# Scan of a hybrid encoder block: log dt in the exponential's bias with an additive mask, weights made a slot ahead, reordered slot, native fp32 state products, first tap on ScalarE

## The chip, the cores and the metric

The kernel runs on one core of a Trainium2 chip. The metric is device time in microseconds (us). Engines are named as in the profile: PE (TensorE's matmuls; PEld is its weight loads), DVE (VectorE), ACT (ScalarE), POOL (GpSimd), SP (SyncE, which only issues DMAs here). SBUF is the on-chip working memory, PSUM the banks into which PE writes.

## The reference, cut to what matters

One encoder block: a combined input projection of 1024 tokens, then a Hyena branch, a Mamba-2 (SSD) branch and gates, their mixing and a mixture of experts. The change touches only the SSD branch and the projection loop around it:

```python
xbc = silu(centred_dwconv(p_xbc, conv_w, conv_b))          # 5 taps; xs, B, C
dt = softplus(p_dt + dt_bias)                               # (l, 2 directions, 32 heads)
a = dt * -exp(a_log)
# per direction, in 8 chunks of 128 tokens, 8 groups of 4 heads:
A_cs = cumsum(a)                                            # within a chunk
decay = exp(where(tril, A_cs[l] - A_cs[s], -inf))
y_diag = einsum(CB[l, s], decay[l, s], (xs * dt)[s])        # CB = C . B
states = einsum(B, exp(A_cs[-1] - A_cs), xs * dt)
carry = carry * chunk_decay + states                        # over the chunks
y_off = einsum(C, carry, exp(A_cs))
y = y_fwd + y_bwd + xs * d_skip;  y = y * silu(z), then an RMS norm per group
```

The Hyena projections pass through a centred convolution of 3 taps.

## The kernel before

The part in question is the function `front`, the first 1436 us. It runs over 89 **units**, each a projection of 128 columns of `w_in` (one of 64): `dt`, then for each of 8 SSD **groups** `xs0`, `xs1`, `B`, `C` (convolved), `z0`, `z1`, and between them 24 `hy` and 16 `gate` units. One unit is one **slot**. In it `proj_cm` runs 8 steps k, each of 6 matmuls of 512 columns in the reduced format fp32r (weights hi and lo by data hi and lo); `hook(k)` puts other matmuls ahead of step k. The order of every engine is written out by hand (a manual schedule): each engine runs its instructions in the order in which the code emits them. The scan of a group runs in slots of the following group: `start[g] = b` is its first slot, and `at(slot, when, f)` hangs a piece of work at a step k or at "begin", "side" (after the projection) or "end".

For chunk c, `pe1(c)` at step 4 of slot b+2+c makes C.B into bank S, the chunk's state from the weighted `xw`, and into bank O the product of C with the two carried states, as three fp32r products of 512 columns (`mm3`) of split operands (`sR`, `Chl`). `side_a(c)` after the projection masks C.B (`cbm`), advances the forward state `sF`, splits it, builds the exponent `Em` on DVE from `bcs` (the running sums A, broadcast by a DMA) and takes the exponential on ACT; POOL then multiplies the masked C.B by dt for both directions, head by head (`Wm`), adds the two, makes `yt` = xs * d and, last, weighs the next chunk's `xw` (`weigh`). `side_b` multiplies the weights by the exponential. `pe3(c)` at step 7 of the next slot applies them into bank Y, and `side_c(c)` at the begin of slot b+4+c sums the terms up. `post` convolves the unit before on DVE (`pin` to `acc...`), and `w_split` prepares the next unit's weights: `whi` on ACT, `wlo` on POOL.

At a group's end `post1` and `post2` normalise `zs` (8 scalings on ACT), transpose it and store it. Groups 1, 3 and 5 have 10 slots, the others 11, so `post2` falls into different slots of the next group. Three slots in a row, start[g] to start[g]+2, hold it together with the next group's transposes (`t1`, `t2`, `zs_tr`) and its backward states (`back`); they are called the **boundary** below, and the slots from start[g]+3 to the group's last its **middle**. Bank tags and their buffers: A (projections) 4, S 1, O 2, Y 1.

## Time and profile before

| | us |
|---|---|
| median of 3 runs (lowest 3528.78, highest 3532.55) | 3530.07 |
| the profiled execution, its time | 3534.84 |
| its span, first to last instruction | 3533.2 |

| share of the span | PE | PEld | DVE | ACT | POOL |
|---|---|---|---|---|---|
| busy | 90% | 71% | 73% | 40% | 47% |

The profiled execution is 4.8 us above the median, and 1.6 us of its time lie outside its span. [...]

### The profile page before, as it was taken

The numbers are of one execution on the slowest core, as the hardware profiler recorded it, in microseconds if no ns is written. First come the engines' busy times: TensorE is split into PE (matmuls) and PEld (weight loads), VectorE is DVE, ScalarE is ACT, GpSimd is POOL, SyncE is SP. The second block draws the span as 40 slices with busy tenths as digits, with TensorE's granted clock in tenths as the row PEclk, the third lists the DMA queues.
The fourth block names the chain that finished last, engine by engine and source line by source line (L and its number), as shares of the span: only waits on it lengthen the run. The fifth ranks groups of instructions, "written<-read, shape, count | busy, mean of one in ns | idle before, by whom it ended". The sixth has DMA issues, their size and how long they took to land. (4 is left out here: it accounts for less than half of the span.)

```text
span 3533.2 us, 42386 instructions
## 1 busy us (share of the span) xinstructions
PE 3188.0 (90%) x14923; PEld 2506.6 (71%) x14923; DVE 2590.6 (73%) x3551; ACT 1406.7 (40%) x2206; POOL 1676.7 (47%) x1480
## 2 busy tenths in 40 slices
PE   8989998989998998899999999997889888888893
PEld 6767776777777777567888888875666666666662
DVE  6787887888787878557994344657778787677786
ACT  3334333343334232322223212415656555565663
POOL 2545454555454546441110320215667667777774
PEclk9999899999999999899999999988999999899996
DMA  4323232322322322744325445327999899888894
GB/s 131 78 72 87 67 96 75 85 73 79 91 78 75 89 72 91 215 147 151 106 90 173 126 155 158 107 85 242 271 271 270 259 259 262 250 249 249 250 283 128
DMA packets 439908, 538.22 MB, mean 152 GB/s; under 512 B 24361, under 2 KB 373325, under 8 KB 430989
## 3 DMA queue, kind: packets, MB, share of 16 engines
q1 hardware_dynamic: 404717, 379.23, 36.6%
q0 software_dynamic: 33824, 152.06, 15.0%
q10 hardware_dynamic: 1152, 4.19, 0.3%
q8 instruction: 119, 1.95, 0.2%
q14 instruction: 96, 0.79, 0.1%
HBM read 430.29 MB, written 105.12 MB: 152 GB/s over the span
## 5 line engine op out<-in xcount | busy, mean ns | idle before, releaser
L170 PE MATMUL bankA<-xth,whi 128*128 128x512 f32 (+1 forms) x1424 | 470.1, 412 | 0.5 <-ACT whi L73 0.3
L170 PE MATMUL bankA<-xtl,whi 128*128 128x512 f32 (+1 forms) x1424 | 452.6, 400 | 0.0
L170 PE MATMUL bankA<-xth,wlo 128*128 128x512 f32 (+1 forms) x1424 | 449.4, 397 | 1.5 <-POOL wlo L74 1.5
L1618 DVE TENSOR_TENSOR elo<-eraw,ehi 128x2048 fp32r<-128x2048 f32 (+1 forms) x134 | 393.7, 2945 | 18.9 <-ACT ehi L1611 13.1
L1661 POOL DMA_INDIRECT scr_acc<-yo,sidx x96 | 231.1, 2407 | 275.9 <-DMA scr_acc<-yo,sidx 147.1
L1611 ACT CAST ehi<-eraw 128x2048 fp32r<-128x2048 f32 (+1 forms) x198 | 356.3, 1852 | 3.3 <-DMA eraw<-in_exp_w_gate_dram 3.3
L74 POOL TENSOR_TENSOR wlo<-wraw,whi 128x1024 fp32r<-128x1024 f32 (+1 forms) x89 | 225.4, 2532 | 278.1 <-ACT whi L73 278.1
L170 PEld LDWEIGHTS bankA<-xtl,whi 128*128 128x128 f32 (+1 forms) x1424 | 274.5, 193 | 64.1 <-DVE xtl L74 0.4
L170 PEld LDWEIGHTS bankA<-xth,wlo 128*128 128x128 f32 (+1 forms) x1424 | 272.2, 191 | 64.5 <-POOL wlo L74 2.0
L170 PEld LDWEIGHTS bankA<-xth,whi 128*128 128x128 f32 (+1 forms) x1424 | 268.2, 195 | 58.3 <-issue 5.4
L1618 POOL TENSOR_TENSOR elo<-eraw,ehi 128x2048 fp32r<-128x2048 f32 x64 | 298.1, 4658 | 15.8 <-ACT ehi L1611 14.7
L399 POOL TENSOR_SCALAR Wm<-cbm,dt 128x128 f32<-128x128 f32 x256 | 129.9, 507 | 348.2 <-DVE cbm L373 348.2
L1625 POOL DMA_INDIRECT xg<-scr_h,gidx x96 | 182.3, 1899 | 63.4 <-issue 24.3
L79 PE MATMUL bankA<-elo,xgh 128*128 128x512 f32 (+1 forms) x512 | 203.6, 398 | 8.6 <-DVE elo L1618 8.6
L78 PE MATMUL bankA<-ehi,xgh 128*128 128x512 f32 (+1 forms) x512 | 210.1, 410 | 0.0
L80 PE MATMUL bankA<-ehi,xgl 128*128 128x512 f32 (+1 forms) x512 | 203.3, 397 | 0.0
L1640 PE MATMUL bankB<-ident,xg 128*128 128x128 f32 (+3 forms) x768 | 113.4, 295 | 94.0 <-DMA xg<-scr_h,gidx 92.5
L1640 PEld LDWEIGHTS bankB<-ident,xg 128*128 128x128 f32 (+3 forms) x768 | 101.5, 198 | 122.9 <-issue 107.5
L74 DVE TENSOR_TENSOR xgl<-bankB,xgh 128x512 fp32r<-128x512 f32 (+1 forms) x128 | 81.3, 664 | 107.7 <-ACT xgh L73 106.0
L80 PE MATMUL bankA<-ehi,hb 128*128 128x512 f32 (+1 forms) x256 | 121.3, 474 | 27.0 <-DVE hb L74 26.9
L1877 DVE SCALAR_TENSOR_TENSOR lows<-lows,wt 64x256 f32<-64x256 f32 (+1 forms) x32 | 132.5, 4140 | 15.5 <-ACT lows L1876 15.5
L393 DVE SCALAR_TENSOR_TENSOR Em<-bcs,Acs,Em 128x128 f32<-128x128 f32 x256 | 140.9, 609 | 2.3
(551 smaller groups left out, 7672.7 us busy)
## 6 DMA issues: line engine op xcount, KB each, us to landing
eraw<-in_exp_w_gate_dram SPq DMA_DIRECT2D x128, 512.0 KB, 5.9
eraw<-in_exp_w_down_dram POOLq DMA_DIRECT2D x64, 1024.0 KB, 6.0
eraw<-in_exp_w_up_dram SPq DMA_DIRECT2D x128, 512.0 KB
wraw<-in_w_in_dram SPq DMA_DIRECT2D x88, 512.0 KB, 4.1
bcs<-scr_at SPq DMA_DIRECT2D x128, 256.0 KB, 5.6
scr_K<-kout SPq DMA_DIRECT2D x32, 512.0 KB, 2.8
Kt<-scr_K SPq DMA_DIRECT2D x32, 512.0 KB, 3.5
scr_gate<-accf SPq DMA_DIRECT2D x16, 512.0 KB, 4.2
```

Of the source, the lines that this page charges most:

```text
L74: (lo_eng or nc.vector).tensor_tensor(lo, src, hi.bitcast(F32), ALU.subtract)
L78: mm(out, sh, mh, start=first, stop=False)
L79: mm(out, sh, ml, start=False, stop=False)
L80: mm(out, sl, mh, start=False, stop=last)
L170: mm(ps[h], wt[:, k, :n], x[:, h * 512:(h + 1) * 512], start=(k == 0 and f == 1), stop=(k == KT - 1 and l == 1))
L393: STT(E[:, h], bcs[:, 1, h], self.A[:, c, 32 + j:33 + j], E[:, h], ALU.subtract, ALU.min)
L1611: nc.scalar.copy(whl[p][0][:, c], wraw[p][:, c])
L1618: eng.tensor_tensor(lo[:, c], wraw[p][:, c], hi[:, c].bitcast(F32), ALU.subtract)
L1625: nc.gpsimd.indirect_dma_start(out=t[:n, :], out_offset=None, in_=self.h_d, in_offset=bass.IndirectOffsetOnAxis(ap=tabs[r][s][0], axis=0))
L1640: nc.tensor.transpose(ps[:, j * P:j * P + n], free(t[:n, k:k + 1], [[8, P]]), self.ident[:n, :n])
L1661: nc.gpsimd.indirect_dma_start(out=self.acc_d, out_offset=bass.IndirectOffsetOnAxis(ap=tabs[r][s][1], axis=0), in_=y[:n, :], in_offset=Non ...
L1877: nc.vector.scalar_tensor_tensor(t[:, 0:256], t[:, 0:256], w, t[:, 256:512], ALU.mult, ALU.mult)
```

## The change

1. **dt by its logarithm.** `atr` makes A' = log(dt) corrected - A once (`self.A`). Per chunk, `side_e` adds a mask `negm` (0 or -1e30) to the broadcast sums of both directions in one DVE instruction of 1024 columns, and ACT takes eight exponentials of 128 columns (four heads, two directions) with A' as bias. The weights are E0 + E1 (`side_a`), times C.B straight from bank S (`side_b`). POOL's eight multiplications by dt and their sum, the masked C.B and the DVE exponent are gone.
2. **A slot ahead.** `side_e(c)` and `side_a(c)` run in slot b+1+c, one before `pe1(c)`; `weigh` runs two chunks ahead; `bcs` is loaded one slot earlier.
3. **Native state product.** `pe1` multiplies C by the states in plain fp32, two products of 256 columns, without splits.
4. **Reordered slot.** `post` is a generator in three pieces: the first tap (now on ACT, `AF.Identity`) or the tanh ahead of the slot, the other taps after the projection's hooks, the last SiLU product after the side work. `wlo` is made on POOL where the unit before has 5 taps, otherwise on DVE.
5. xs * d is made once per group on ACT; both `off` products are one instruction; for groups 1, 3 and 5 the second `post2` moves from the next slot's step 1 to the "side" of its own.

```diff
-        self.split(raw[:, :, :n], hi[:, :, :n], lo[:, :, :n], self.nc.gpsimd)
-        return hi, lo
+        self.nc.scalar.activation(hi[:, :, :n], raw[:, :, :n], AF.Copy)
+        return hi, lo, raw
+
+    def w_low(self, w, eng, n=P):
+        hi, lo, raw = w
+        eng.tensor_tensor(lo[:, :, :n], raw[:, :, :n], hi[:, :, :n].bitcast(F32), ALU.subtract)
...
-        nc.vector.tensor_scalar(acc, pin[:, 0:L], wcols[0], bcol, ALU.mult, ALU.add)
+        nc.scalar.activation(acc, pin[:, 0:L], AF.Identity, bias=bcol, scale=wcols[0])
+        yield
...
+            TS(c3(x), self.dt, 1e-18, None, ALU.max)
+            nc.scalar.activation(e, x, AF.Ln)
+            nc.scalar.activation(s, e, AF.Exp, scale=-1.0)
+            TT(s, s, x, ALU.mult)
+            STT(e, s, -1.0, e, ALU.add, ALU.add)
+            TT(self.A, c3(e), self.A, ALU.subtract)
...
             weigh(0, 0)
-            load_bc(0)
+            weigh(1, 0)
...
+            S["y"] = pool.tile([P, 8, 256], F32, name="yt", bufs=1)
+            y4, x4 = [v.rearrange("p c (h q) -> p h c q", q=64) for v in (S["y"], S["X"])]
+            for h in range(4):
+                nc.scalar.activation(y4[:, h], x4[:, h], AF.Copy, scale=self.drow[:, 4 * g + h:4 * g + h + 1])
...
-            v = slice(0 if c > 0 else 256, 512 if c < 7 else 256)
-            self.mm3(po[:, v], S["c"][:, 0], S["c"][:, 1], S["R"][:, 0, v], S["R"][:, 1, v], True, True)
+            if c > 0:
+                nc.tensor.matmul(po[:, 0:256], tl["C"][:, tok], S["sF"], start=True, stop=True)
+            if c < 7:
+                nc.tensor.matmul(po[:, 256:512], tl["C"][:, tok], S["st"][:, c + 1], start=True, stop=True)
...
+        def side_e(c):
+            E = S["bcs", c]
+            v = self.negm
+            TT(E, E, bass.AP(v.tensor, v.offset, [list(v.ap[0]), [P, 2], [0, 4], [1, P]]), ALU.add)
+            for d in range(2):
+                for h in range(4):
+                    j = d * 32 + 4 * g + h
+                    nc.scalar.activation(E[:, d, h], E[:, d, h], AF.Exp, bias=self.A[:, c, j:j + 1])
+            if c < 7:
+                load_bc(c + 1)
+
         def side_a(c):
-            cs = S["cs"]
-            cbm = pool.tile([P, 2, P], F32, name="cbm", bufs=1)
-            v = cs[:, 0:P]
-            TT(cbm, bass.AP(v.tensor, v.offset, [list(v.ap[0]), [0, 2], [1, P]]), self.mask, ALU.mult)
+            E = S.pop(("bcs", c))
+            M = S.setdefault("M", {})[c] = pool.tile([P, 4, P], F32, name="Wm", bufs=3)
+            TT(M, E[:, 0], E[:, 1], ALU.add)
+
+        def side_b(c):
+            cs, M = S["cs"], S["M"][c]
...
-                r_split(S["R"], sF, 0, nc.vector)
-                if c < 6:
-                    r_split(S["R"], S["st"][:, c + 2], 1, nc.vector)
-                c_split(c + 1)
-            E = pool.tile([P, 4, P], F32, name="Em", bufs=2)
-            bcs = S["bcs"]
-            TT(E, bcs[:, 0], hb(self.A, c, 0, P), ALU.subtract)
-            for h in range(4):
-                j = 4 * g + h
-                STT(E[:, h], bcs[:, 1, h], self.A[:, c, 32 + j:33 + j], E[:, h], ALU.subtract, ALU.min)
-            nc.scalar.activation(E, E, AF.Exp)
...
-                nc.gpsimd.tensor_scalar(W[:, h], cbm[:, 0], self.dt[:, c, j:j + 1], 0.0, ALU.mult, ALU.add)
-                nc.gpsimd.tensor_scalar(W2[:, h], cbm[:, 1], self.dt[:, c, 32 + j:33 + j], 0.0, ALU.mult, ALU.add)
-            GT(W, W, W2, ALU.add)
...
-            if c < 6:
-                weigh(c + 1, 0)
...
-        def side_b(c):
-            W = S["W"]
-            TT(W, W, S["E"], ALU.mult)
-            S["M"][c] = W
+                    TT(S["sF"], tf, cs[:, P:P + 256], ALU.add)
+            v = cs[:, 0:P]
+            TT(M, M, bass.AP(v.tensor, v.offset, [list(v.ap[0]), [0, 4], [1, P]]), ALU.mult)
+            if c < 5:
+                weigh(c + 2, 0)
...
+            d0, d1 = 1 if c == 0 else 0, 1 if c == 7 else 2
+            e = self.eA[:, c, 4 * g:4 * g + 4]
+            e = bass.AP(e.tensor, e.offset + 32 * d0, [list(e.ap[0]), [32, d1 - d0], [1, 4], [0, 64]])
...
+            TT(o4[:, d0:d1], p4[:, d0:d1], e, ALU.mult)
...
+                    tl[i][kind] = t
+                    yield
+                    yield
                     STT(t, th, 1.0, t, ALU.add, ALU.mult)
-                    tl[i][kind] = t
...
+                at(b, "end", lambda j=j: j["load_bc"](0))
                 for c in range(8):
+                    at(b + 1 + c, "first", lambda j=j, c=c: j["side_e"](c))
                     at(b + 2 + c, 4, lambda j=j, c=c: j["pe1"](c))
-                    at(b + 2 + c, "side", lambda j=j, c=c: j["side_a"](c))
                     at(b + 2 + c, "side", lambda j=j, c=c: j["side_b"](c))
+                for c in range(8):
+                    at(b + 1 + c, "side", lambda j=j, c=c: j["side_a"](c))
                     at(b + 3 + c, 7, lambda j=j, c=c: j["pe3"](c))
                     at(b + 4 + c, "begin", lambda j=j, c=c: j["side_c"](c))
...
-                    at(b + 11 + q, 7 - 6 * q, f)
+                    if q and g in FILL4:
+                        at(b + 11, "side", f)
+                    else:
+                        at(b + 11 + q, 7 - 6 * q, f)
...
+                taps = pend is not None and units[pend[0]][0] in ("xs0", "xs1", "B", "C")
+                if u + 1 < len(units) and (taps or u < 2):
+                    self.w_low(ws[u + 1], nc.gpsimd, width(u + 1))
...
+                step = post(*pend) if pend is not None else iter(())
+                next(step, None)
+                run(u, "first")
                 run(u, "begin")
+                if u + 1 < len(units) and not (taps or u < 2):
+                    self.w_low(ws[u + 1], nc.vector, width(u + 1))
...
-                if pend is not None:
-                    post(*pend)
-                    pend = None
+                next(step, None)
...
+                if not last:
+                    run(u, "side")
+                    for _ in step:
+                        pass
```

On POOL, one slot of the before (the last pair of the eight multiplications by dt, up to the weights' low part), in the middle of group 2: `Wm` are weights, `xw` the weighted data that `pe1` of the next slot waits for.

```order
L399 TENSOR_SCALAR Wm<-cbm,dt 128x128
L400 TENSOR_SCALAR Wm_2792<-cbm,dt 128x128
L401 TENSOR_TENSOR Wm<-Wm,Wm_2792 128x512
L405 TENSOR_TENSOR yt<-Xtok,drow 128x256
L301 TENSOR_TENSOR xw<-Xtok,wst 128x256
L564 MEMSET pin 128x2
L565 MEMSET pin 128x2
L74 TENSOR_TENSOR wlo<-wraw,whi 128x1024
```

After the change POOL's rows at the same kind of place are these (several slots in one piece):

```order
L163 TENSOR_TENSOR wlo<-wraw,whi 128x1024
L312 TENSOR_TENSOR xw<-Xtok,wst 128x256 x2
L555 MEMSET pin 128x1
L556 MEMSET pin 128x1
L312 TENSOR_TENSOR xw<-Xtok,wst 128x256
```

Between two weighings of `xw` there is no longer any row that waits for PE's bank S through `cbm`.

On DVE, the scan's rows of one slot before, after the projection, in a middle (up to the next slot's first product):

```order
L373 TENSOR_TENSOR cbm<-bankS,mask 128x256
L381 TENSOR_TENSOR tf<-sF,cdec 128x256
L382 TENSOR_TENSOR sF<-tf,bankS 128x256
L74 TENSOR_TENSOR sR<-sF,sR 128x256
L74 TENSOR_TENSOR sR<-st,sR 128x256
L74 TENSOR_TENSOR Chl<-accC,Chl 128x128
L390 TENSOR_TENSOR Em<-bcs,Acs 128x512
L393 SCALAR_TENSOR_TENSOR Em<-bcs,Acs,Em 128x128 x4
L414 TENSOR_TENSOR Wm<-Wm,Em 128x512
L425 TENSOR_TENSOR off<-bankO,eA 128x256 x2
```

And one whole slot after the change, where the unit before was a gate:

```order
L378 TENSOR_TENSOR bcs<-bcs,negm 128x1024
L415 TENSOR_TENSOR off<-bankO,eA 128x512
L416 TENSOR_TENSOR yt<-yt,bankY 128x256
L418 TENSOR_TENSOR yt<-yt,off 128x256 x2
L420 TENSOR_TENSOR zs<-yt,zs 128x256
L163 TENSOR_TENSOR wlo<-wraw,whi 128x1024
L399 TENSOR_TENSOR tf<-sF,cdec 128x256
L400 TENSOR_TENSOR sF<-tf,bankS 128x256
L402 TENSOR_TENSOR Wm<-Wm,bankS 128x512
L389 TENSOR_TENSOR Wm<-bcs 128x512
```

The exponent and the splits have left, and `wlo` and the wide mask addition have come; the weights of the next chunk (the last row) stand behind those of this one.

On ACT, the second slot of the boundary behind group 1 before: `pin` is the evacuated projection, the eight `zs<-zs,rs` are `post1`'s scalings, and the `Xtok` copies empty the banks of `t2`'s transposes.

```order
L567 ACTIVATE pin<-bankA,par 128x512 x2
L73 ACTIVATE whi<-wraw 128x1024
L433 ACTIVATE off,ss<-zs 128x256
L442 ACTIVATE zs<-zs,rs 128x256 x8
L280 COPY Xtok<-bankO 128x4x128
L280 COPY Xtok<-bankS 128x4x128
L280 COPY Xtok<-bankY 128x4x128
L450 ACTIVATE zs<-bankS,par 128x4x128
```

The same slot after the change:

```order
L558 ACTIVATE pin<-bankA,par 128x512 x2
L158 ACTIVATE whi<-wraw 128x1024
L180 ACTIVATE accC<-pin,parh 128x1024
L382 ACTIVATE bcs<-bcs,Acs 128x128 x8
L421 ACTIVATE off,ss<-zs 128x256
L430 ACTIVATE zs<-zs,rs 128x256 x8
L291 COPY Xtok<-bankO 128x4x128
L291 COPY Xtok<-bankS 128x4x128
L291 COPY Xtok<-bankY 128x4x128
L438 ACTIVATE zs<-bankS,par 128x4x128
```

The first tap and the eight exponentials now stand ahead of the scalings and of the copies.

## Rows read from the trace of the kernel before

Lines are those of the kernel before; the middles run from 129.83 to 249.51, 300.84 to 411.49, 468.35 to 587.20, 641.27 to 749.87, 802.62 to 925.23, 976.61 to 1085.24, 1140.97 to 1257.69 and 1310.36 to 1404.40 us (the last without its final slot), the boundaries between them.

**Rows 1.** the first line of the page
```profile
span 3533.2 us, 42386 instructions
```

**Rows 2.** busy time by engine (us, instructions), granted PEclk, DMA: the front
```profile
16.47:1436.00 1419.53, 1296.64 (x5856) 1042.07 (x5853) 1132.67 (x1747) 499.53 (x929) 721.55 (x985) 0.94 0.31 84
```

**Rows 3.** who waited for whom on PE, 129.83 to 1404.40 (us, times, longest)
```profile
PE bankS L356 <- POOL xw L301: 34.8, 12, 5.3
PE bankS L449 <- ACT zs L442: 21.7, 4, 6.8
PE bankO L78 <- DVE off L425: 14.7, 27, 1.3
```

**Rows 4.** timeline of PE at unit 33: start, us, engine, line [idle before]
```profile
537.40 1.22 PE L356 MATMUL bankS<-xw,Btok 128*128 128x256 f32 x2 [4.50 <-POOL xw L301]
```

**Rows 5.** timeline of POOL in the same stretch
```profile
530.79 0.47 POOL L399 TENSOR_SCALAR Wm<-cbm,dt 128x128 f32<-128x128 f32 x1 [9.68 <-DVE cbm L373]
```

**Rows 6.** windows: the eight middle stretches, first, last and their sum
```profile
129.83:249.51 119.68, 112.05 (x508) 90.98 (x507) 102.64 (x156) 39.57 (x73) 66.15 (x98) 0.96 0.33 84
...
1310.36:1404.40 94.04, 85.69 (x388) 69.61 (x387) 83.68 (x117) 24.63 (x51) 60.83 (x89) 0.96 0.28 84
...
sum 899.78, PE 833.08 PEld 675.47 DVE 774.47 ACT 290.40 POOL 506.66; mean PE 104.14 PEld 84.43 DVE 96.81 ACT 36.30 POOL 63.33
```

**Rows 7.** windows: a slot in which PE never waits, and unit 33's
```profile
548.60:561.90 13.30, 13.30 (x64) 11.10 (x64) 12.12 (x20) 4.78 (x9) 4.20 (x8) 1.00 0.42 95
527.02:548.60 21.58, 17.00 (x66) 13.03 (x65) 17.94 (x31) 6.43 (x14) 14.67 (x22) 0.84 0.26 74
```

**Rows 8.** windows: boundaries behind groups 0, 2, 4 and 6, first and sum
```profile
249.51:300.84 51.33, 46.49 (x214) 37.24 (x213) 34.76 (x56) 22.50 (x40) 20.27 (x20) 0.93 0.30 73
...
sum 209.45, PE 187.40 PEld 150.18 DVE 141.64 ACT 91.08 POOL 80.53; mean PE 46.85 PEld 37.54 DVE 35.41 ACT 22.77 POOL 20.13
```

**Rows 9.** windows: boundaries behind groups 1, 3 and 5, first and sum
```profile
411.49:468.35 56.86, 49.34 (x223) 39.86 (x222) 38.78 (x69) 24.44 (x44) 25.44 (x32) 0.91 0.26 65
...
sum 165.34, PE 144.70 PEld 117.18 DVE 118.00 ACT 72.59 POOL 73.55; mean PE 48.23 PEld 39.06 DVE 39.33 ACT 24.20 POOL 24.52
```

**Rows 10.** groups by line, DVE, 111.67 to 1436
```profile
L393 DVE SCALAR_TENSOR_TENSOR Em<-bcs,Acs,Em 128x128 f32<-128x128 f32 x256 | 140.9, 609 | 2.3
L430 DVE TENSOR_TENSOR yt<-yt,off 128x256 f32<-128x256 f32 x112 | 136.1, 1215 | 3.9
L390 DVE TENSOR_TENSOR Em<-bcs,Acs 128x512 f32<-128x512 f32 x64 | 45.1, 705 | 0.0
L600 DVE SCALAR_TENSOR_TENSOR accxs<-pin,accxs 128x1024 f32<-128x1024 f32 x14 | 17.2, 1226 | 16.9 <-ACT pin L599 16.9
```

**Rows 11.** groups by line, POOL, 111.67 to 1436
```profile
L74 POOL TENSOR_TENSOR wlo<-wraw,whi 128x1024 fp32r<-128x1024 f32 x81 | 205.2, 2533 | 215.5 <-ACT whi L73 215.5
L399 POOL TENSOR_SCALAR Wm<-cbm,dt 128x128 f32<-128x128 f32 x256 | 129.9, 507 | 348.2 <-DVE cbm L373 348.2
```

**Rows 12.** groups by line, ACT, 111.67 to 1436
```profile
L73 ACT ACTIVATE whi<-wraw 128x1024 fp32r<-128x1024 f32 x81 | 85.5, 1055 | 0.0
L442 ACT ACTIVATE zs<-zs,rs 128x256 f32<-128x256 f32 x64 | 26.5, 496 | 27.5 <-DVE rs L473 27.5
L73 ACT ACTIVATE Chl<-accC 128x128 fp32r<-128x128 f32 x64 | 18.9, 295 | 0.0
```

**Rows 13.** timeline of PE: native matmuls of 256 columns, then fp32r of 512
```profile
445.54 0.59 PE L317 MATMUL bankS<-xw,Btok 128*128 128x256 f32 x2
445.97 0.59 PE L317 MATMUL bankY<-xw,Btok 128*128 128x256 f32 x2
...
528.39 0.62 PE L170 MATMUL bankA<-xth,whi 128*128 128x512 f32 x2
528.85 0.62 PE L170 MATMUL bankA<-xtl,whi 128*128 128x512 f32 x2
```

**Rows 14.** the tile bcs: time from issue to landing of its loads
```profile
DMA to landing us min/median/max: 4.7/5.6/10.2
```

More of the change, by code (lines that the diff above doesn't have):

```diff
@@ L342, in load_bc @@
                 nc.sync.dma_start(bcs[:, d], bass.AP(s.tensor, s.offset, [[0, P], [L, 4], [1, P]]))
-            S["bcs"] = bcs
+            S["bcs", c] = bcs
         def zs_tr(q):
@@ L426, in side_c @@
             TT(y, y, py[:, 0:256], ALU.add)
-            for d in range(2):
-                if (d == 0 and c == 0) or (d == 1 and c == 7):
-                    continue
+            for d in range(d0, d1):
                 TT(y, y, off[:, d], ALU.add)
@@ L451, in post2 @@
             return lambda: nc.sync.dma_start(self.yss_d[g * 256 + q * P:g * 256 + (q + 1) * P, :].rearrange("p (j t) -> p j t", t=P), yo)
-        return dict(states1=states1, t1x=t1x, t1=t1, t2=t2, states=states, zs_tr=zs_tr, pe1=pe1, pe3=pe3, side_a=side_a, side_b=side_b,
+        return dict(load_bc=load_bc, states1=states1, t1x=t1x, t1=t1, t2=t2, states=states, zs_tr=zs_tr, pe1=pe1, pe3=pe3, side_e=side_e, side_a=side_a, side_b=side_b,
                     side_c=side_c, post1=post1, post2=post2)
@@ L501, in front @@
                 nc.sync.dma_start(self.mask, a["c_tri"])
+                self.negm = pp.tile([P, 2, P], F32, name="negm")
+                nc.vector.tensor_scalar(self.negm, self.mask, 1e30, -1e30, ALU.mult, ALU.add)
                 for i, _ in enumerate(xt):
@@ L579, in post @@
                     acc = wp.tile([P, L], F32, name="accf", bufs=2)
-                    self.conv(t, acc, 3, [self.pcol(self.c_hcw, k * 24 + i) for k in range(3)], self.pcol(self.c_hcb, i))
+                    yield from self.conv(t, acc, 3, [self.pcol(self.c_hcw, k * 24 + i) for k in range(3)], self.pcol(self.c_hcb, i))
                     if i >= 16:
@@ L593, in post @@
                     acc = sq.tile([P, L], F32, name="acc" + kind, bufs=1)
-                    self.conv(t, acc, 5, [self.hcol(self.c_scw, k * 32 + r) for k in range(5)], self.hcol(self.c_scb, r))
+                    yield from self.conv(t, acc, 5, [self.hcol(self.c_scw, k * 32 + r) for k in range(5)], self.hcol(self.c_scb, r))
                     tl[i][kind] = acc
@@ L603, in post @@
                     else:
-                        silu()
+                        yield from silu()
             slots = {}
@@ L682, in front @@
                     next(self.flt)
-                run(u, "side")
+                if not last:
+                    run(u, "side")
+                    for _ in step:
+                        pass
                 run(u, "end")
```

51 lines of the change are left out of this document (15 added, 36 removed).

## The prediction

> **What bounds the kernel now.** The change lies in the front, so I first asked what that stage costs. The span is 3533.2 us [rows 1]; the front takes 1419.5 of it, and in it PE is busy for 1296.6 us at a granted clock of 0.94 [rows 2]. PE is therefore the bound, and it loses time in two ways: 122.9 us idle, and about 0.06 of the stretch, 85 us, because half-speed stretches do half the work. No other engine comes near: DVE has 1132.7 us, POOL 721.6, ACT 499.5 [rows 2]. What a change here can win is what PE loses by waiting; what follows the front only moves.
>
> Who makes PE wait: in the table of waits POOL's `xw` leads with 34.8 us in 12 waits, then the scalings of `zs` on ACT with 21.7 in 4, and `off` on DVE with 14.7 in 27 small ones [rows 3]. One of them in the timeline: in unit 33 PE sits idle 4.50 us for `xw` [rows 4], and POOL had itself sat 9.68 us for `cbm` [rows 5], because DVE convolves xs1 before it masks C.B, and `xw` is the last row of POOL's slot. That slot lasts 21.58 us at a clock of 0.84, against 13.30 us at 1.00 for a slot in which PE never waits [rows 7]. So a wait of 4.5 us costs 8.3: after it PE runs at the lower level for a while.
>
> I cut the front by groups. The eight middles, 59 slots, last 899.8 us with PE busy for 833.1, at clocks of 0.94 to 0.97 (first and last 0.96) [rows 6]: 66.7 us idle and, at a mean of about 0.955, 38 us of clock. Check: 59 slots at 13.3 are 785; the 115 left are these 104 and heavier slots.
>
> **The change, part by part.**
>
> PE's own work. A native 256-column product takes 0.43 us from start to start, a pair of fp32r products of 512 columns 0.46, so 0.23 each [rows 13]. Per chunk three of the latter (0.69) become two of the former (0.86): +0.17 for 48 chunks, less (about 0.08) for the 16 end chunks: **+9.5 us**. This work is on the path.
>
> The middle's waits. `xw` is now weighed two chunks ahead and POOL no longer passes through `cbm`: its weights in both directions (129.9 us for one, about as much for the other) and their sum leave it, and of its 89 `wlo` instructions of 2533 ns each, 54 go to DVE [rows 11]. Behind `xw`, what is late next is `off`, which frees bank O at step 4, about 5.5 us into a slot. So DVE must keep up. It loses the exponent, 140.9 + 45.1 = 186 us [rows 10], and, not counted here, the splits, `cbm` and the first taps. It gains 64 mask additions of 1024 columns, 64 sums of 512 and 54 `wlo`. For 1024 columns no such row exists: the lower bound is 1226 ns (L600), the upper POOL's 2533 ns; for 512 columns 705 ns (L390) [rows 10, 11]. I take the lower one, as it is the same engine and width: 78 + 45 + 66 = 189 us, so DVE's load stays about even before the uncounted parts come off; at the upper bound it grows by 155, to some 1290 us, all of the time that the front would have left. Against this, `yt` (256 columns) averages 1215 ns where 512 columns take 705 [rows 10]: DVE is held up while POOL runs, and POOL's load falls by more than half. Besides, the masked C.B no longer starts a chain on POOL; a late `side_b` has until step 7 of the next slot. Hence I forecast no lasting wait in the middles.
>
> ACT gains eight exponentials of 128 columns per chunk, bounded by 295 ns (a 128-column copy) and 414 ns (26.5 us over 64 scalings of 256 columns) [rows 12]: 2.4 to 3.3 us instead of one of 0.6, and 56 first taps near the 1055 ns of `whi` [rows 12]. ACT is busy for 290 of the 900 us of the middles [rows 6]; 64 x 2.7 + 59 = 232 us more at most fit. What a taps slot needs in all (evacuation, `whi`, tap, exponentials, square, tanh) is about 7.5 us of 13.3.
>
> [...]
>
> So the middles give back 66.7 + 38 - 9.5 = **95 us**.
>
> The boundaries. Behind groups 0, 2, 4 and 6 they take 209.5 us, with PE idle for 22.0 and clocks of 0.90 to 0.93 (17 us): 42.5 us each without waits [rows 8]. Behind groups 1, 3 and 5 it is 165.3, 20.6 idle and 11.6 of clock, 44.4 each without [rows 9]. Here not all comes back, since ACT's order has new rows ahead of the copies that empty PE's banks. First kind: in the first slot the scalings are ready earlier and PE's wait for them goes; in the second ACT does evacuation, `whi`, first tap and exponentials, some 7 us, before it copies bank S, which PE wants again after 5.4: 2 us of wait and about as much of clock; in the third the four `yt` scalings (at most 0.83 each, twice a 414 ns row) cost about 1.3. I leave 5.2, so 47.7 each and **19 us** won. Second kind: first tap and exponentials push the eight scalings and the copies behind them back by 3.5 to 4.4 us, and PE meets bank S at step 7: 4.5 of wait, 2 of clock, 1 in the next slot: 51.8 each, **10 us** won. `log(dt)` adds some 5 short instructions once; `bcs`'s wait for it lies two slots later: nothing.
>
> Sum: 95 + 19 + 10 = 124 us. The profiled execution took 3534.84; less 124 it is 3410.8, and scaled by 3530.07 / 3534.84, **3406 us**, which is 3.5% less.
>
> **The rivals.**
>
> *Half comes back.* The ACT queue hurts more than I count: the boundaries win nothing (29 us) and the three slots behind each wait 1.3 us more with as much of clock (24 x 1.5 = 35 us). For it: PE already waits for `zs` copies [rows 3], and ACT is strictly in order. Against: ACT's low load. That leaves 60 us: 3530 - 60 = **3470** (3440 to 3500). It decides where an exponential takes 0.6 us instead of 0.3: that pushes each copy behind eight of them by 2.4 us. [...]
>
> *More comes back.* DVE and ACT are so early that the boundaries are clean too: their 42.6 us idle and 29 us of clock come back, not 29: 124 + 42 = 166, so **3364**.
>
> *Slower.* The mask addition is the first DVE row of a slot and waits for a DMA, `bcs`. If it lands late, DVE stands, `off` is late, and PE waits in each of 56 slots. It is issued at the begin of the slot before and lands after 5.6 us, at most 10.2 [rows 14], in 13.3. From a landing of 13.3 us on PE begins to wait; to lose the 124 us again it takes 2.2 us more per slot, a landing of 15.5; at 16 us it is 2.7 x 56 = 151 us, and the kernel stands at 3530 - 124 + 151 = **3557**. Against it: no landing comes near, with DMA busy for 0.31 of the front [rows 2].
>
> *The change does not do what it says.* If `xw` early only uncovers another wait (`off`, `sF`) of the same length, the middles win a third (32 us) and the boundaries nothing: about **3498**; the small 0.5 us waits for `off` speak for it, DVE's load after the change against it.
>
> **How the numbers follow.** A measurement of this kernel tells about 0.2%, 7 us, from no change. Forecast (3380 to 3440) 0.56; half 0.20; more 0.12; uncovered wait 0.06, most of it still faster; slower 0.06. Range: from the clean boundaries to past the middle of "half", 3363 to 3475. Faster 0.92, same 0.02, slower 0.06.
>
> **What would show it.** Right: middles near 805 us in sum with no wait for `xw`, clock above 0.98; the DVE share of the front near 75%; PE's product with the states 0.86 us a chunk; a wait for bank S behind ACT in the second boundary slot of 2 us, or 4 to 5 behind groups 1, 3 and 5. Wrong: waits of PE for `off` or `sF` in the middles (DVE late), exponentials above 0.5 us, a mask addition above 2 us, or `bcs` landing after 13 us.

## The result, and the profile after

The changed kernel takes **3427.35 us** (median of 4 runs, 3420.95 to 3431.94) where the kernel before, run beside it, takes 3529.43: a ratio of **0.9715, 95% interval 0.9686 to 0.9745**. Forecast were 3406 us, with a range of 3363 to 3475. The profiled execution has a span of 3430.3 us, 102.9 less than [rows 1]; the forecast sum was 124.

The same cut of the front as before shows where it went. First the windows of the changed kernel: the eight middles (first, last, sum), the boundaries of the first kind (first, sum), of the second (first, sum), and a slot in which PE never waits, with the columns of [rows 2].

```profile
149.50:256.75 107.25, 107.25 (x513) 89.39 (x512) 73.54 (x103) 51.18 (x103) 13.93 (x17) 1.00 0.34 86
...
1225.06:1306.44 81.38, 81.38 (x393) 68.43 (x392) 61.76 (x81) 37.08 (x85) 13.38 (x26) 1.00 0.30 93
sum 795.06, PE 795.06 PEld 663.88 DVE 554.88 ACT 376.89 POOL 112.26; mean PE 99.38 PEld 82.99 DVE 69.36 ACT 47.11 POOL 14.03
...
256.75:310.52 53.77, 45.38 (x214) 36.76 (x212) 28.49 (x49) 28.58 (x56) 10.94 (x15) 0.94 0.35 84
...
sum 213.09, PE 182.88 PEld 147.77 DVE 113.69 ACT 114.66 POOL 43.85; mean PE 45.72 PEld 36.94 DVE 28.42 ACT 28.66 POOL 10.96
...
405.88:455.44 49.56, 46.21 (x222) 37.35 (x220) 31.53 (x56) 30.87 (x59) 11.20 (x15) 0.97 0.37 82
...
sum 148.79, PE 138.68 PEld 112.34 DVE 97.43 ACT 93.29 POOL 33.78; mean PE 46.23 PEld 37.45 DVE 32.48 ACT 31.10 POOL 11.26
...
483.91:497.32 13.41, 13.41 (x65) 11.27 (x64) 9.10 (x14) 7.47 (x16) 0.00 (x0) 1.00 0.29 79
```

The middles went from 899.8 to 795.1 us [rows 6]: PE is busy for all of it at a granted clock of 1.00 (the profile gives it as a share of full speed), and DVE's share of them fell from 774 to 555 us. The boundaries of the second kind won 16.6 us [rows 9]; those of the first lost 3.6 [rows 8].

Where PE still waits, from the table of waits between 133 and 1330 us, and then in the first 133:

```profile
PE bankS L290 <- ACT zs L438: 25.6, 8, 6.9
PE bankS L437 <- ACT Xtok L291: 7.3, 3, 2.5
```

```profile
PE bankA L145 <- DVE xtl L74: 18.1, 2, 17.9
...
PE bankS L290 <- DVE accB L594: 3.6, 1, 3.6
```

No wait for `xw` or `off` is left [rows 3]. But the first projection product starts at 35.2 us instead of 16.5, and unit 7 at 133.05 instead of 111.67: **21.4 us lost at the start**, which the prediction had at nothing. The account by stretches: start +21.4, the boundary slot behind it (16.45 us against 18.16) -1.7, middles -104.7, first kind +3.6, second kind -16.6, from unit 88 on -4.9: -102.9, the whole difference of the spans. In all profiles shown here of the changed kernel and its variants the part behind unit 88, which no edit touches, lies between 2116 and 2128 us; so below I compare stretches of the front where a few microseconds matter.

The rows that the prediction priced, from the groups of DVE between 133 and 1330 us, and of ACT:

```profile
L183 DVE SCALAR_TENSOR_TENSOR accxs<-pin,parh,accxs 128x1024 f32<-128x1024 f32 x56 | 91.0, 1625 | 53.2 <-ACT accxs L180 50.7
L378 DVE TENSOR_TENSOR bcs<-bcs,negm 128x1024 f32<-128x1024 f32 x63 | 76.8, 1219 | 50.5 <-DMA bcs<-scr_at 49.9 <-DMA scr_S<-frn 0.6
L163 DVE TENSOR_TENSOR wlo<-wraw,whi 128x1024 fp32r<-128x1024 f32 x53 | 64.6, 1219 | 28.0 <-ACT whi L158 28.0
...
L418 DVE TENSOR_TENSOR yt<-yt,off 128x256 f32<-128x256 f32 x112 | 53.0, 473 | 3.9
L389 DVE TENSOR_TENSOR Wm<-bcs 128x512 f32<-128x512 f32 x63 | 46.0, 731 | 0.0
```

```profile
L180 ACT ACTIVATE accf<-pin,par 128x1024 f32<-128x1024 f32 x24 | 29.7, 1239 | 0.0
```

The mask addition took 1.22 us, the lower bound taken; the sum 0.73. `yt` fell from 1215 ns to 473 [rows 10]. The first tap on ACT took 1.24 us, not the 1055 ns of `whi` [rows 12].

### The profile page after: what moved, and what is told of

It reads as the page before. It is cut to its first block, busy times and chain, and to the rows that moved or that the text cites. A ratio compares the mean times of both kernels' runs of the same rounds, so it can differ in the third digit from the quotient of the medians.

```text
span 3430.3 us, 41518 instructions
## 1 busy us (share of the span) xinstructions
PE 3140.6 (92%) x14954; PEld 2488.9 (73%) x14955; DVE 2316.2 (68%) x3074; ACT 1549.7 (45%) x2570; POOL 1182.6 (34%) x786
## 5 line engine op out<-in xcount | busy, mean ns | idle before, releaser
L174 PE MATMUL bankA<-xtl,whi 128*128 128x512 f32 (+1 forms) x1424 | 445.5, 394 | 0.0
L1633 DVE TENSOR_TENSOR elo<-eraw,ehi 128x2048 fp32r<-128x2048 f32 (+1 forms) x134 | 395.2, 2956 | 18.8 <-ACT ehi L1626 12.3
L163 POOL TENSOR_TENSOR wlo<-wraw,whi 128x1024 fp32r<-128x1024 f32 (+1 forms) x35 | 83.4, 2383 | 646.3 <-ACT whi L158 646.3
L1633 POOL TENSOR_TENSOR elo<-eraw,ehi 128x2048 fp32r<-128x2048 f32 x64 | 297.3, 4645 | 16.6 <-ACT ehi L1626 10.1
L558 ACT ACTIVATE pin<-bankA,par 128x512 f32<-128x512 f32 x112 | 71.1, 687 | 327.9 <-PE bankA L174 327.6
L382 ACT ACTIVATE bcs<-bcs,Acs 128x128 f32<-128x128 f32 x512 | 156.4, 392 | 39.8 <-DVE bcs L378 39.7
```

What stands on the lines that cost most here:

```text
L163: eng.tensor_tensor(lo[:, :, :n], raw[:, :, :n], hi[:, :, :n].bitcast(F32), ALU.subtract)
L174: mm(ps[h], wt[:, k, :n], x[:, h * 512:(h + 1) * 512], start=(k == 0 and f == 1), stop=(k == KT - 1 and l == 1))
L382: nc.scalar.activation(E[:, d, h], E[:, d, h], AF.Exp, bias=self.A[:, c, j:j + 1])
L1633: eng.tensor_tensor(lo[:, c], wraw[p][:, c], hi[:, c].bitcast(F32), ALU.subtract)
```

## The experiments

Each edit is to the changed kernel unless it says "kernel before". Ratios are to the kernel before, run beside it on the same chip; the changed kernel's is 0.9715.

**The start: negm behind the splits.** In the changed kernel DVE's third row is this one:

```profile
25.86 0.29 DVE L491 TENSOR_SCALAR negm<-mask 128x256 f32<-128x256 f32 x1 [24.62 <-DMA mask<-in_c_tri_dram]
26.07 3.22 DVE L74 TENSOR_TENSOR xtl<-bankA,xth 128x512 fp32r<-128x512 f32 x5
```

```diff
-                nc.vector.tensor_scalar(self.negm, self.mask, 1e30, -1e30, ALU.mult, ALU.add)
                 for i, _ in enumerate(xt):
...
+            nc.vector.tensor_scalar(self.negm, self.mask, 1e30, -1e30, ALU.mult, ALU.add)
```

> The changed kernel, with the one VectorE row that makes negm from the mask moved behind the sixteen splits of the transposed input (it was third in DVE's queue). Theory: in the changed kernel that row waits 24.6 us for the mask's DMA, which SP issues last of the parameters, and the splits stand behind it, so PE's first projection product starts at 35.2 us instead of 16.5. Then the first product starts near 17 us here, and the span falls by 16 to 19 us, to about 3412-3414 us. Rival: the start is late because the transfers themselves land later, or the loss moves to the next wait (the weights' split on POOL, the parameters' transposes): then the first product comes at 25 us or later and less than 8 us are won.

Measured: 3419.29 us, ratio 0.9678 (0.9653 to 0.9703). The first projection product starts at 16.53 us, 18.7 earlier, so the cause is the late mask. But unit 5 starts only 14.8 earlier: the first two units take 28.0 us instead of 24.0, with waits of 1.1 and 1.5 us for `whi` and `wlo`. The span is 12.2 us shorter: the size was off, between the two forecasts, for the most part because some 4 us of the loss had hidden the weights' splits. The interval of the ratio overlaps that of the changed kernel, so the size rests on the traces.

**The boundaries of the first kind: the load of bcs.** Timelines of the changed kernel behind group 0: SP, ACT and PE.

```profile
268.30 0.54 SPq L439 DMA_DIRECT2D scr_yss<-zs  x1
268.89 1.87 SPq L346 DMA_DIRECT2D bcs<-scr_at  x2
```

```profile
273.09 1.24 ACT L180 ACTIVATE accC<-pin,parh 128x1024 f32<-128x1024 f32 x1
280.42 2.45 ACT L382 ACTIVATE bcs<-bcs,Acs 128x128 f32<-128x128 f32 x8 [6.09 <-DVE bcs L378]
282.78 0.67 ACT L438 ACTIVATE zs<-bankS,par 128x512 f32<-128x512 f32 x1
```

```profile
283.50 1.11 PE L290 MATMUL bankS<-ident,accxs 128*128 128x128 f32 x4 [6.94 <-ACT zs L438]
```

SP issues `bcs` only behind the store of `yss`, which waits 18.3 us for ACT, by SP's own waits from 250 to 275 us:

```profile
SPq L439 <- ACT zs L438: 18.3, 1, 18.3
```

DVE stands 13.3 us for it, the eight exponentials stand for DVE, the copy that empties bank S stands behind them on ACT, and PE stands 6.94 us for bank S. Two edits take the chain apart at different links. The first loads early:

```diff
-                at(b, "end", lambda j=j: j["load_bc"](0))
+                at(b, "first", lambda j=j: j["load_bc"](0))
```

> The changed kernel, with the first bcs load of each group issued at the head of slot b (before the store of the previous group's yss, which waits on SP for ACT's scaled copies) instead of at its end. Theory: at the boundaries behind groups 0, 2, 4 and 6 the late load is the cause of the wait of PE: bcs lands at 279, the eight exponentials start late, and the copies out of bank S stand behind them on ACT. With the load early, DVE's wait for bcs (49.9 us in 4 waits) goes to under 4 us in all, PE's wait for bank S in the second slot falls from 5.5-6.9 to about 2 us (the 2 us of the prediction), and the four boundaries fall from 213 us to 190-198: 15 to 23 us off the span. Rival: ACT's order alone is the cause (eight exponentials, first tap and split ahead of the copies, whenever they start): then DVE's wait goes, PE's stays above 4.5 us, and under 6 us are won.

Measured: 3397.54 us, ratio 0.9615 (0.9592 to 0.9638). The four boundaries take 185.3 us, 27.8 less, where 15 to 23 were forecast. DVE's wait for `bcs` is 0.2 us, and the exponentials follow the first tap at once:

```profile
272.77 1.24 ACT L180 ACTIVATE accC<-pin,parh 128x1024 f32<-128x1024 f32 x1
273.91 2.44 ACT L382 ACTIVATE bcs<-bcs,Acs 128x128 f32<-128x128 f32 x8
276.25 0.67 ACT L438 ACTIVATE zs<-bankS,par 128x512 f32<-128x512 f32 x1
```

PE's wait there is 0.7 us. The order on ACT is unchanged and costs almost nothing: the late load was the cause.

The second edit leaves the load late and moves the exponentials behind the copies:

```diff
-                    at(b + 1 + c, "first", lambda j=j, c=c: j["side_e"](c))
+                    at(b + 1 + c, "first" if c else 4, lambda j=j, c=c: j["side_e"](c))
```

> The changed kernel, with the mask addition and the eight exponentials of chunk 0 of each group moved from the head of slot b+1 to its step 4, behind the copies that empty PE's banks (and behind DVE's work of the last chunk); the load stays late. Theory of a queue: PE waits for bank S at the boundaries because the copies stand behind the exponentials on ACT; with them behind the copies, the waits of 5.5-6.9 us behind groups 0, 2, 4, 6 and of 2.4 us behind 1, 3, 5 both go, and the sum of the seven boundaries falls by 20 to 30 us. Rival: late bcs only meets another reader, the sum of the two halves on DVE at the slot's end and the taps in front of it (DVE stands at bcs until 280 us all the same), so silu and the products of the next slot are late and under 8 us are won.

Measured: 3406.07 us, ratio 0.9633 (0.9607 to 0.9659). The first kind fell to 194.9 us, the second stayed at 148.2: 18.8 less in the seven, a little under the forecast, and the second kind's wait halved (7.3 to 3.7 us) without shortening it. DVE still stands 49.7 us for `bcs` in 4 waits, and PE now waits 7.4 us in 3 for `st`, which stands behind it. So the queue on ACT passes the lateness on, but the lateness comes from the load; mending the load gives more.

**One chunk of lead for xw.**

```diff
-            weigh(1, 0)
...
-            if c < 5:
-                weigh(c + 2, 0)
+            if c < 6:
+                weigh(c + 1, 0)
```

> The changed kernel, with xw weighed one chunk ahead (at the end of the slot before its product) instead of two; nothing else of the slot is touched. Theory: what freed the middles is that POOL no longer stands behind DVE's mask of C.B and the weights' chain, so a slot is lead enough: no xw waits above 1 us, the middles' sum within 5 us of 795, the time the same within 0.2%. Rival: the second chunk of lead is what does it, since POOL's split of the weights (2.4 us) and DVE's taps still stand ahead of xw: then the waits of 3 to 5 us for xw come back in the slots with taps (12 waits, 35 us with as much of clock again), and the kernel is 30 to 70 us slower than the changed one.

Measured: 3424.80 us, ratio 0.9696 (0.9671 to 0.9722); middles 795.1 us. The second chunk of lead is worth nothing, in the middles or in the time (the intervals overlap).

**The kernel before, with xw first on POOL.** This asks whether `xw`, the wait on which the prediction began, was the bound of the middles.

```diff
         def side_a(c):
+            if c < 6:
+                weigh(c + 1, 0)
             cs = S["cs"]
...
-            if c < 6:
-                weigh(c + 1, 0)
```

> The kernel before, with one thing moved: xw of the next chunk is the first row of POOL's part of a slot, ahead of the weights' chain that waits for cbm, instead of the last. Theory: the place of xw behind the chain is what makes PE wait in the middles, so this move alone takes the 12 waits (34.8 us) and the clock behind them (4.5 us of wait cost 8.3): the middles fall from 899.8 to 830-850 us, the time by 50 to 70 us. Rival: with xw early the chain itself is next (the weights' sum and the product with the exponent come too late for PE's step 7 of the next slot), or DVE, which is busy for 774 of the 900 us there and late with off and sF: then PE waits for Wm, off or sF instead, the middles stay above 875 and under 25 us are won.

Measured: 3528.88 us, ratio 0.999 (0.9979 to 1.0001): no difference, and the rival holds. PE's waits, 130 to 1442 us:

```profile
PE bankO L78 <- DVE off L425: 76.1, 30, 6.4
```

The table of the kernel before has one more line for the matmul that reads `xw`, between the lines of [rows 3]:

```profile
PE bankS L356 <- POOL pin L565: 15.4, 10, 2.6
```

`pin` is the row right behind `xw` on POOL, and in each of these waits PE starts as `xw` ends; so it waited for `xw` for 34.8 + 15.4 = 50.2 us, in 22 waits. They are gone, and those for `off` went from 16.2 (same window) to 76.1; the middles still take some 899 us (a few records of PE are missing here and in the run below, so the starts of slots are read to one or two us). DVE's timeline around unit 33, the place of [rows 4]:

```profile
525.20 0.80 DVE L176 TENSOR_SCALAR accxs<-pin,parh 128x1024 f32<-128x1024 f32 x1
526.03 5.32 DVE L178 SCALAR_TENSOR_TENSOR accxs<-pin,parh,accxs 128x1024 f32<-128x1024 f32 x4
532.56 1.23 DVE L600 SCALAR_TENSOR_TENSOR accxs<-pin,accxs 128x1024 f32<-128x1024 f32 x1 [1.21 <-ACT pin L599]
...
537.28 2.46 DVE L395 SCALAR_TENSOR_TENSOR Em<-bcs,Acs,Em 128x128 f32<-128x128 f32 x4
540.50 0.69 DVE L414 TENSOR_TENSOR Wm<-Wm,Em 128x512 f32<-128x512 f32 x1 [0.77 <-ACT Em L396]
541.12 0.75 DVE L425 TENSOR_TENSOR off<-bankO,eA 128x256 f32<-128x256 f32 x2
```

From one `off` (520.41) to the next it is 20.7 us, 17.8 of them busy and the rest short waits, the named ones all for ACT, where a slot without waits lasts 13.3. `off` frees bank O, and PE stands for it 5.6 us:

```profile
542.01 0.77 PE L78 MATMUL bankO<-sR,Chl 128*128 128x512 f32 x1 [5.64 <-DVE off L425]
```

**The kernel before, with the slot reordered.** Is it then the order on DVE, or its load?

```diff
+                if not last:
+                    run(u, "side")
                 if pend is not None:
                     post(*pend)
...
-                run(u, "side")
+                    run(u, "side")
```

(The last added line stands under `if last:`.)

> The kernel before, with one thing moved: a slot's work on its chunk (cbm, sF, the splits, the exponent, the weights) is written ahead of the convolution of the projected tile instead of behind it. It is the reordered slot alone, with every row as long as before. It follows from the run with xw first, where the waits for xw went and waits for off on DVE (73.7 us in 29) took their place, so that nothing was won. Theory of the order: DVE's taps (7.4 us with the square and its wait) stand ahead of cbm, which starts POOL's chain, and ahead of off; behind them nobody waits soon. So the waits for xw and for off go together, the middles fall from 899.8 to 800-840 us and 50 to 90 us are won. Theory of the load: in a slot with five taps DVE's rows are 19.6 us end to end, and the slot 13.3; whatever comes last is late for the next slot, so off is late again (or the silu behind the taps), the middles stay above 870, and the cheaper exponent, not the order, is what the change won by.

Measured: 3550.82 us, ratio 1.0044 (1.0030 to 1.0059): no gain, and some 0.4% longer. The middles take some 936 us, the boundaries some 18 less than before. PE's waits, 130 to 1442 us, and DVE ahead of one of them, in which PE stands 3.13 us until 581.18:

```profile
PE bankO L78 <- DVE off L425: 95.3, 34, 4.9
```

```profile
574.94 0.81 DVE L176 TENSOR_SCALAR accf<-pin,par 128x1024 f32<-128x1024 f32 x1
575.78 4.59 DVE L178 SCALAR_TENSOR_TENSOR accf<-pin,par,accf 128x1024 f32<-128x1024 f32 x2
580.29 0.74 DVE L425 TENSOR_TENSOR off<-bankO,eA 128x256 f32<-128x256 f32 x2
```

`xw` no longer waits, but now the taps stand right ahead of `off`. With rows as long as before, both orders tried are late with `off`. So the theory of the order falls, and the middles stay above 870 as the theory of the load says; its last part, that the cheaper exponent is what the change won by, this run does not show.

**Parts given back to the changed kernel, one at a time.** All `wlo` on POOL:

```diff
-                if u + 1 < len(units) and (taps or u < 2):
+                if u + 1 < len(units):
                     self.w_low(ws[u + 1], nc.gpsimd, width(u + 1))
...
-                if u + 1 < len(units) and not (taps or u < 2):
-                    self.w_low(ws[u + 1], nc.vector, width(u + 1))
```

> The changed kernel, with all 89 wlo on POOL (54 of them were on DVE at 1.22 us each; on POOL they take 2.4). Theory: with no POOL chain left and DVE at about 9.5 of 13.4 us in a clean slot, neither engine is near PE, so it makes no difference: middles within 5 us of 795, time within 0.2% of the changed kernel. Rival: DVE and POOL slow each other (the taps on DVE take 1.63 us beside POOL's wlo where they took 1.32 before), so more POOL work makes DVE's rows longer and off late: middles 10 us or more above 795. A second rival, faster: 66 us off DVE bring the boundaries, where DVE is late, 10 us down.

The first tap back on DVE:

```diff
-        nc.scalar.activation(acc, pin[:, 0:L], AF.Identity, bias=bcol, scale=wcols[0])
         yield
+        nc.vector.tensor_scalar(acc, pin[:, 0:L], wcols[0], bcol, ALU.mult, ALU.add)
```

> The changed kernel, with the first tap of each convolution back on VectorE (0.80 us there before, 1.24 us on ACT in the changed kernel). Theory: DVE has room in the middles now, so they stay within 4 us of 795; at the boundaries ACT has 1.2 us less ahead of the copies that empty bank S, so the seven of them fall by 3 to 8 us and the kernel is 0.1 to 0.25% faster than the changed one. Rival: in the slots with taps DVE's rows are the ones that end last, so 0.8 us more on DVE make off or the silu late, and middles and boundaries grow by 10 us or more: then the first tap on ACT was a needed part.

The state product as three fp32r products with their splits, as the kernel before has it:

```diff
...
-            if c > 0:
-                nc.tensor.matmul(po[:, 0:256], tl["C"][:, tok], S["sF"], start=True, stop=True)
-            if c < 7:
-                nc.tensor.matmul(po[:, 256:512], tl["C"][:, tok], S["st"][:, c + 1], start=True, stop=True)
+            v = slice(0 if c > 0 else 256, 512 if c < 7 else 256)
+            self.mm3(po[:, v], S["c"][:, 0], S["c"][:, 1], S["R"][:, 0, v], S["R"][:, 1, v], True, True)
...
```

> The changed kernel, with the state products as before: three fp32r products of 512 columns with C, the running state and the next state split in two (Chl and sR; Chl and sF have one buffer here, to fit), instead of native fp32 products. It asks what that part of the change costs or gives by itself. Theory by the prediction's term: where PE never waits only PE's work counts, 0.17 us less per chunk, so the middles fall from 795 to about 787 and the splits (2.0 us of DVE and 1.1 of ACT per chunk) hide. Rival: the way from the product with xw over sF, ACT's copy and DVE's rest back to PE's next state product is as long as a slot again, and DVE goes from 9.5 to 11.5 us of a 13.4 us slot: PE waits for sR or off, the middles grow by 10 to 50 us, and the native products, dearer on PE, pay for themselves by what they take off DVE and ACT.

The sums of the eight middles in the three, in this order:

```profile
sum 795.09, PE 795.09 PEld 663.88 DVE 568.88 ACT 377.27 POOL 196.52; mean PE 99.39 PEld 82.99 DVE 71.11 ACT 47.16 POOL 24.57
```

```profile
sum 795.00, PE 795.00 PEld 664.15 DVE 611.47 ACT 327.70 POOL 129.26; mean PE 99.38 PEld 83.02 DVE 76.43 ACT 40.96 POOL 16.16
```

```profile
sum 788.02, PE 787.57 PEld 654.27 DVE 595.81 ACT 417.38 POOL 113.20; mean PE 98.45 PEld 81.78 DVE 74.48 ACT 52.17 POOL 14.15
```

- `wlo`: 3445.22 us, ratio 0.9753 (0.9740 to 0.9765). The middles don't move, as the theory says, but the seven boundaries take 16.7 us more (225 and 154 us), which neither theory had; both rivals fall. (The intervals of the two times just overlap.) In the trace PE's waits for the `zs` copies on ACT rise from 3.0 to 11.7 us and those of its transposes in bank S for `st` on DVE from 1.2 to 4.7; why POOL's longer queue brings them about was not followed up.
- First tap: 3431.99 us, ratio 0.9700 (0.9679 to 0.9721). Middles and time as in the changed kernel, boundaries 0.6 us less in sum (first kind 1.5 more, second 2.1 less): DVE has room for it, and ACT for it too. The 3 to 8 us forecast for the boundaries did not come; in the first kind ACT waits for `bcs`, whatever stands ahead.
- Native products: 3441.45 us, ratio 0.9739 (0.9727 to 0.9752). In the middles fp32r is 7.0 us quicker (8 forecast). The boundaries are 15.2 us longer: PE's waits for the `zs` copies on ACT in the third slot rise from 3.0 to 18.4 us, for ACT's splits of the first chunk stand ahead of them. So by the traces native fp32 pays, by 8 us, though not where its cost was weighed; the intervals of the two times overlap.

**log(dt) a slot later.**

```diff
             at(4, 6, dt[3])
+            at(5, "begin", dt[4])
```

(`dt[4]` holds the rows of `log(dt)` from `atr`.)

> The changed kernel, with the five rows of log(dt) and the new A moved from slot 4, step 6, to the head of slot 5. Theory: in slot 4 DVE stands 2.6 us behind ACT's Ln and Exp (two table loads of 1.28 us among them), the taps and silu of B come late behind it, and PE waits 3.6 us for accB in slot 5, which lasts 19.1 us. Moved, the wait goes, and slot 5 lasts 13 to 15 us: 4 to 6 us off the front, 0.1 to 0.2% off the time. Rival: DVE is late in slot 4 anyway (evacuations for the transposed A and B's five taps), and the chain only takes its time from the next slot: slot 5 and 6 together stay within 2 us of 33.1.

Measured: 3430.11 us, ratio 0.9700 (0.9685 to 0.9715): in the time it can't be told. In the trace slot 5 falls from 19.1 to 14.8 us and slots 5 and 6 together from 33.1 to 28.8: the wait for `accB` goes. In its place PE waits 2.2 us in slot 5 for the copy of `Btok`, which by the code's order now stands on ACT behind the two table loads of the Ln and the Exp (1.28 us each in the changed kernel's trace, at 98.60 and 101.52 us). And the slots ahead of them were 1.5 us longer in this profile.

**Together, and without the slot of lead.** The first run joins three edits (negm, early load, log(dt)). The second has them too, but makes the weights in the slot of their chunk:

```diff
-                at(b, "end", lambda j=j: j["load_bc"](0))
+                at(b + 1, "begin", lambda j=j: j["load_bc"](0))
...
-                    at(b + 1 + c, "first", lambda j=j, c=c: j["side_e"](c))
+                    at(b + 2 + c, "first", lambda j=j, c=c: j["side_e"](c))
+                    at(b + 2 + c, "side", lambda j=j, c=c: j["side_a"](c))
...
-                    at(b + 1 + c, "side", lambda j=j, c=c: j["side_a"](c))
```

> The changed kernel, with three edits together: negm behind the splits of the input, the first bcs load of a group at the head of slot b, log(dt) at the head of slot 5. Theory: the three lie at different places of the front and add up: by slot 7 some 14 to 17 us are won, the four boundaries behind groups 0, 2, 4 and 6 take 185 instead of 213 us, the middles stay at 795, and the time is 42 to 48 us below the changed kernel, 3382 to 3388 us. Rival: they overlap (an early start meets weights that land late, an early slot 5 waits for log(dt) anyway): 30 us or less, above 3397 us.

> As the run with the three edits, but mask addition, exponentials and the sum of the two directions are made in the slot of their chunk instead of a slot ahead (bcs of chunk 0 loaded a slot later). Against that run it tells what the slot of lead is worth. Theory: it is worth nothing in the middles: the mask addition and the exponentials at a slot's head take some 4 us, the sum and the product come at its end, and PE wants the weights at step 7 of the next slot: middles within 5 us of 795, and the boundaries within 10 us, since the exponentials leave one slot and go to the next. Rival: the mask addition is on DVE behind the taps of the slot before, the exponentials wait for it and the sum for them, and copies on ACT stand behind: PE waits for off or for Wm, and the middles grow by 20 us or more.

Measured: 3383.52 us, ratio 0.9579 (0.9559 to 0.9600), as forecast, though the three don't quite add up. By unit 7 14.5 us are won, where the edit of negm alone wins 13.8: that of log(dt) gives less than 1 us here. Slot 5 lasts 17.2 us, and in it PE waits 3.78 us for `Btok`, which by the code's order stands behind the table loads:

```profile
101.25 0.66 PE L292 MATMUL bankS<-ident,accxs 128*128 128x128 f32 x4 [3.78 <-ACT Btok L293]
```

The boundaries of the first kind win 27.7 us, and of the 48.4 us by which the span is shorter 4.4 lie behind unit 88, where no edit acts.

Without the slot of lead 3378.34 us, ratio 0.9560 (0.9539 to 0.9581): in the time the two can't be told apart. In the traces the middles stay (795.2 and 796.3 us), and the boundaries are 8.5 us shorter in sum without the lead (180.9 and 143.2 against 185.3 and 147.2); a likely reason, not tested apart, is that the exponentials leave the slot in which ACT also empties PE's banks. With these edits the slot of lead is worth nothing. Both are faster than the kernel before by over 4%, and their intervals lie below that of the changed one.

## Why the prediction was right, and where not

**Middles, 95 forecast, 104.7 measured.** The size came from what PE lost there (idle and clock), and all of it came back: 795 us where 805 were forecast. The clock is 1.00, as said, and the clean slot 13.41 us against 13.30 [rows 7], +0.11 where +0.17 was forecast for PE's own work. Where the other 10 us come from the run with three fp32r products tells: with that product as before and next to no waits the middles last 788.0, so the kernel before lost 111.8 us there, 7 more than the 66.7 + 38 of the sum, and the native products cost 7.0 in the middles, not 9.5.

What bound the middles was put too narrowly: `xw` was only the first to be late. Putting it early left the time as it was, because `off` took its place, which was the rival "uncovered wait", on the kernel before. DVE's own waits say which engine was behind. The largest for PE in the kernel before (111 to 1436 us) and in the changed one (133 to 1330):

```profile
DVE st L319 <- PE bankO L317: 4.2, 4, 1.2
```

```profile
DVE yt L416 <- PE bankY L372: 69.6, 33, 4.1
```

Before, DVE never waits for PE directly in a middle: its rows take 774 of the 900 us, 13.1 a slot, and its waits for ACT and POOL another 109, so its queue was full. After, its rows take 555, 9.4 a slot, and it waits for PE. The prediction had this as a condition ("DVE must keep up") and counted the load as about even, naming splits, `cbm`, first taps and POOL's hold on DVE without counting them. DVE's share of the front was to be near 75%; it is 66 (35.19 to 1306.44 us), and 70 in the middles.

Not settled is which of DVE's rows, or of its waits for ACT and POOL, had to go. Giving back `wlo`'s place, the first tap (DVE then at 611 us) or the splits one at a time brings no wait of note back into the middles, nor does one chunk less of lead for `xw` or, with the other edits, the slot of lead. What no run gave back is the exponent with POOL's weights' chain, which belong together; that it is the part that counts is what remains, not what was shown. Nor were several parts given back at once.

**First kind of boundary, -19 forecast, +3.6 measured.** The failing step is the load's: the prediction took every `bcs` as "issued at the begin of the slot before", and the first of a group stands at a slot's end, behind a store on SP that waits for ACT. With that one row moved the four take 46.3 us each, where 47.7 were forecast, and the wait for bank S is 0.7 us and not 2. The rival "slower" had the mechanism, a late `bcs`, but in every slot and not in four.

**Second kind, -10 forecast, -16.6 measured.** The wait for bank S in its second slot is 2.4 us, not 4.5.

**Start, 0 forecast, +21.4 measured.** The term that was missing, not mis-sized: negm, a row of 0.29 us, was not priced at all, and log(dt) was called "nothing". The late negm puts the first product off by 18.7 us, of which some 4 hide the first weights' splits. With log(dt) slots 5 and 6 take 33.1 us where the kernel before takes 26.6: 6.5 more, 3.6 of them the wait for `accB`, most of the others clock (0.83 in slot 5). Together these are the 21.4. Both edits gave back 14.5 by unit 7; of the 6.9 left 5.1 lie in slots 5 and 6, where PE now waits 3.78 us for `Btok`, behind the rows of log(dt) by the code's order.

**Prices.** The mask addition lay at its lower bound, and eight exponentials took 2.45 us (2.4 to 3.3 forecast). The first tap took 1239 ns where 1055 stood: 184 ns more. It has two operands given as a column of 128 values each, scale and bias, which `whi` has not; whether they make the difference no run shows. That one exponential of 512 columns became eight of 128 decided nothing here: once they start on time PE waits at most 0.7 us behind them in the boundaries of the first kind.

**Two slips.** The prediction read the table of waits without the line of `pin`, so `xw` had 50.2 us and not 34.8; no term of the sum hangs on it. And 1.3 us of wait with as much of clock are 2.6 a slot, 62 us in 24 slots and not 35: by its own terms the rival "half comes back" stood near 3497.

So the forecast came near partly by luck, because errors offset: 10 too little in the middles and 7 in the second kind against 21 at the start and 23 in the first kind.

## What to carry to other kernels

A wait that leads the table names who was last, not who is full: before moving the late row, add up the rows, and the waits, of the in-order engine that feeds it over a run of slots and compare with the slots; and look whether that engine ever waits for the one that it feeds. When a step is moved, ask of each row it issues, even a 0.3 us one that is needed much later, what stands ahead of it and behind it in its queue: here a row that waited 24.6 us for a late DMA, and a DMA whose queue stood 18.3 us for an engine, held everything behind them. Errors at the seams can cost much of what the steady state wins: here 21 us at the start and 23 in the first boundaries, against 105. Moving two rows, negm and the first load, gave most of it back.

## What the runs showed of the hardware

How much longer DVE's rows last beside POOL's `wlo` I had not expected. In the run with xw first, POOL's and DVE's timelines:

```profile
521.88 2.36 POOL L74 TENSOR_TENSOR wlo<-wraw,whi 128x1024 fp32r<-128x1024 f32 x1 [2.29 <-ACT whi L73]
```

```profile
521.52 3.00 DVE L430 TENSOR_TENSOR yt<-yt,off 128x256 f32<-128x256 f32 x2
```

Two additions take 3.00 us here, and end 0.28 us after POOL's instruction does. In the changed kernel's slot from 483.91 to 497.32 us, in which POOL has no row, they take 0.89:

```profile
496.53 0.89 DVE L418 TENSOR_TENSOR yt<-yt,off 128x256 f32<-128x256 f32 x2
```

In the changed kernel `wlo` on POOL (499.58 to 502.00 us), and `xw` behind it, meet the taps instead: four take 6.68 us from 500.67 on, and 5.30 for B's taps at 105.5 us, where POOL is idle. Why the rows last longer no run shows. The trace of the kernel before has both lengths already: its 112 additions of `yt` take 424 to 2583 ns each, 426 in the median, and the pair that starts at 538.92 us beside `wlo` (from 539.14) takes 2.94 us. So the fall of `yt`, to which the prediction gave no size, could have been estimated from it as DVE time won: 112 at 426 ns are 48 us, 88 less than the 136.1 of [rows 10]. Measured, the mean fell from 1215 to 473 ns, 83 us in all.

The clock behind a wait is in the trace of the kernel before, too. After the 4.50 us of unit 33 [rows 4] the granted clock is 0.50 from 538.70 to 542.68 us, where the pairs of fp32r products start 0.85 us apart; from 543.36 to 545.66 it is 1.00, and they start 0.46 apart. So PE did 0.54 of the work there, where the prediction took half.
